# Twelve of 256 elementwise products moved from VectorE to GpSimd in an attention kernel with a bias

## The chip, the cores and the metric

One core of one Trainium2 chip. The metric is device time in microseconds (us) of one execution. A run's time is a little longer than the span of its profile (254.24 against 252.5 in the profiled run of the kernel before), which goes from the first to the last instruction. Engines: TensorE (PE; its weight loads are PEld), VectorE (DVE), ScalarE (ACT), GpSimd (POOL), SyncE (SP).

## The reference

Attention with an additive bias that all heads share: 4 batches x 8 heads, 1024 positions, head size 64.

```
scores = q @ k^T / 8 + bias            # bias: 1 x 1 x 1024 x 1024
attn   = exp(scores - max) / sum(exp(scores - max))
out    = attn @ v
```

## The kernel before

It uses exp(s + bias) = exp(s) * exp(bias). Scores are made transposed (keys on partitions). A *bank* is one block of 128 keys x 512 queries of one head. There are 512 banks in 32 units of 16 (two heads, one half of the queries, eight key blocks). TensorE makes the scores of three banks (one slot), ScalarE takes exp of a slot in one instruction, VectorE multiplies a pair of banks (both heads, same key block) by exp(bias^T), and TensorE forms the weighted sum with v, 65 columns wide so that the last one sums the weights:

```python
def s_fill(g):                                     # TensorE: scores of one slot
    ps = ps_s.tile([P, 3, HQ], F32, tag="s", name="ps")          # two such buffers in PSUM
    for j, b in enumerate(slots[g]):
        ...
        nc.tensor.matmul(ps[:, j, :], kT[:, kc, :], qT[:, h, qh * HQ:(qh + 1) * HQ], start=True, stop=True)

def s_exp(g):                                      # ScalarE
    n = len(slots[g])
    nc.scalar.activation(e_at(slots[g][0], n), open_ps.pop(("S", g))[:, :n, :], ACTF.Exp, scale=scale)

def mul_pair(b, n=2):                              # VectorE: E = E * exp(bias^T), both in SBUF
    pr, h, qh, kc = banks[b]
    e = e_at(b, n)
    nc.vector.tensor_tensor(e, e, eb[:, qh, kc:kc + 1, :].to_broadcast([P, n, HQ]), op=ALU.mult)

def av_bank(b, tag):                               # TensorE: weighted sum
    ...
    for i in range(QC):
        nc.tensor.matmul(acc[:, i, :], e[:, 0, i * P:(i + 1) * P], vall[:, 2 * pr + h, kc, :], ...)
    ...                                            # after 8 banks, VectorE:
        nc.vector.reciprocal(rs[:], acc[:, :, D:D1])                                  # PSUM
        nc.vector.tensor_tensor(oall[...], acc[:, :, :D], rs[:].to_broadcast(...), op=ALU.mult)   # PSUM, SBUF
```

VectorE also copies the transposed q (times a mask) and k out of PSUM. After the start GpSimd only issues loads (of q, k, v and, once, the bias). The order of every engine's instructions is decided when the kernel is built, by a small model of the engines with fixed costs (`EXP` 427 ns a bank, `MUL` 600, and so on). The order is therefore fixed: each engine works through its list, and a wait holds up what stands behind it (in the changed kernel transposes will wait 7.1 us for scalings that stand behind held products).

The softmax here doesn't subtract the row's maximum and nothing guards it: scores larger than these inputs give would overflow.

Of the kernel before, what the change touches and what calls it, by code (L numbers as in the profile page):

```python
# [11 lines left out]
ALU = mybir.AluOpType  # L12
# [3 lines left out]
def kernel(  # L16
# [15 lines left out]
    nc = tc.nc  # L32
    B, H, S, D = q.shape
    P = 128
# [4 lines left out]
    HQ = S // 2  # L39
# [12 lines left out]
    op = ctx.enter_context(tc.tile_pool(name="op", bufs=2))  # L52
# [7 lines left out]
    eb = consts.tile([P, 2, NCH, HQ], BF)  # L60
# [10 lines left out]
    def load_qk(pr):  # L71
        qr = raw.tile([P, 2, NCH, D], BF, name="qr")
        kr = raw.tile([P, 2, NCH, D], BF, name="kr")
        nc.gpsimd.dma_start(out=kr.rearrange("p t c d -> p t (c d)"), in_=kf[pr])  # L74
        nc.gpsimd.dma_start(out=qr.rearrange("p t c d -> p t (c d)"), in_=qf[pr])  # L75
        raws[pr] = (qr, kr)

    def load_v(pr):
        for t in range(2):
            nc.gpsimd.dma_start(out=vall[:, 2 * pr + t, :, :D], in_=vf[pr, :, t])  # L80

    def transpose_pe(pr, which, half, tag):

        src = raws[pr][which]
        px = ps_x.tile([P, QC, P], BF, tag=tag, name="px")
        for c in range(QC):
            for t in range(2):
                nc.tensor.transpose(px[t * D:(t + 1) * D, c, :], src[:, t, half * QC + c, :], ident[:])  # L88
        if (pr, which) not in trs:
            trs[(pr, which)] = (kvp.tile([P, NCH, P], BF, name="kT") if which else  # L90
                                kvp.tile([P, 2, NCH * P], BF, name="qT"))
        dst = trs[(pr, which)]

        def copy():
            if which == 0:

                nc.vector.tensor_tensor(dst[:, :, half * HQ:(half + 1) * HQ],  # L97
                                        px.rearrange("p c q -> p (c q)").unsqueeze(1).to_broadcast([P, 2, HQ]),
                                        mask[:], op=ALU.mult)
            else:  # L100
                nc.vector.tensor_copy(dst[:, half * QC:(half + 1) * QC, :], px[:])  # L101
        return copy


    banks = [(pr, h, qh, kc) for pr in range(NP) for qh in range(2) for kc in range(NCH) for h in range(2)]
# [6 lines left out]
    def e_at(b, n):  # L112
        if b // ET not in etiles:
            etiles[b // ET] = ep.tile([P, ET, HQ], BF, name="E")
        return etiles[b // ET][:, b % ET:b % ET + n, :]
# [26 lines left out]
    def b_exp(qh, k0):  # L142
        nc.scalar.activation(eb[:, qh, k0:k0 + 4, :], open_ps.pop(("B", qh, k0))[:, :4, :], ACTF.Exp)  # L143

    def mul_pair(b, n=2):
        pr, h, qh, kc = banks[b]
        e = e_at(b, n)
        nc.vector.tensor_tensor(e, e, eb[:, qh, kc:kc + 1, :].to_broadcast([P, n, HQ]), op=ALU.mult)  # L148

    oalls = {}  # L150
    po = {}
# [25 lines left out]
    with tc.manual_schedule():  # L177
# [59 lines left out]

        EXP, EXP0, QK, AV, TP = 427, 45, 216, 170, 350
        MUL, COPYQ, COPYK, EVAC, SEM = 600, 650, 420, 620, 80
        order = [("S", g) for g in range(2, NS)]  # L240
        for at, x in ((5, (0, 0)), (7, (0, 4)), (11, (1, 0)), (13, (1, 4))):
            order.insert(at, ("B",) + x)
# [2 lines left out]
        t_act, t_pe, t_dve = T0 + 900, T0, T0  # L245
# [10 lines left out]
        eb_at = {}  # L256
        exp_at = {0: T0 + 400, 1: T0 + 900, 2: T0 + 900}
        mul_at = {}
        mul_next = 0
        av_order = []  # L260
        for u in range(0, NB, 16):
            if u + 16 < NB:
# [5 lines left out]
        def unit_of(b):  # L268
            return banks[b][:3]
# [41 lines left out]
        def pe_piece():  # L311
            if not pieces:
                return None
            pr, which, half = pieces[0]
            if pr not in raw_at or pr not in raws:
                return None
            i = min(len(filled), NO - 1)
            while order[i][0] != "S":
                i -= 1
            at = slots[order[i][1]][0]  # L320
            if at < (pr - 2) * 32 + 8:
                return None

            left = NCH - av_next % NCH
            busy = x_unit.get(unit_of(av_order[av_next])) if av_next % NCH else None
            tags = sorted((x_free[x], x) for x in x_free if x != busy)
            if busy and left < 4 and at < pr * 32 - 16:
                return None
            if not busy and av_next and at < pr * 32 - 16 and tags[0][0] + SEM < t_pe and len(tags) > 1 and tags[1][0] > t_pe:
                return None  # L330
            free, tag = tags[0]
            ready = max(free + SEM, raw_at[pr])

            def emit(t):
                pieces.pop(0)
                copy = transpose_pe(pr, which, half, tag)
                cost = COPYK if which else COPYQ
                x_free[tag] = 1e12

                def run(t2):  # L340
                    copy()
                    x_free[tag] = t2 + cost
                    piece_end[(pr, which, half)] = t2 + cost
                    if which == 0 and half == 1:
                        if pr + 3 < NP:
                            load_qk(pr + 3)
                            raw_at[pr + 3] = t2 + 7000
                        if pr + 2 < NP:
                            load_v(pr + 2)
                dve_q.append((t + TP + SEM, 0, cost, run))  # L350
            return ready, TP, emit

# [27 lines left out]
        def pe_pick():  # L380
            f = pe_fill()
            best = None
            i = len(filled)
            if f and f[0] <= t_pe:
                return (max(t_pe, f[0]),) + f[1:]
            limit = 1e12
            if f:
                limit = max(f[0], act_end_of(i - 1) - f[1] - 100)
            elif i < NO:
                limit = max(act_end_of(i - 2) + SEM, act_end_of(i - 1) - 750)  # L390
            for c in (pe_piece(), pe_av()):
                if c is None:
                    continue
                start = max(t_pe, c[0])
                if start + c[1] > limit:
                    continue
                if best is None or start < best[0]:
                    best = (start,) + c[1:]
            if f and (best is None or f[0] <= best[0]):
                best = (max(t_pe, f[0]),) + f[1:]  # L400
            return best

        def dve_pick():
            nonlocal mul_next
            c = list(dve_q)
            if mul_next < NB:
                pr, h, qh, kc = banks[mul_next]
                if mul_next + 1 in exp_at and (qh, kc) in eb_at:
                    b = mul_next

                    def run(t):
                        nonlocal mul_next
                        mul_pair(b)
                        mul_at[b] = mul_at[b + 1] = t + MUL
                        mul_next += 2
                    c.append((max(exp_at[b + 1], eb_at[(qh, kc)]) + SEM, 2, MUL, run))
            if not c:
                return None
            return min(c, key=lambda x: (max(x[0], t_dve + 100), x[1]))

        def act_pick():
            i = len(act_end)
            if i >= len(filled):
                return None
            return max(t_act, filled[i] + SEM), cost_act(i), i

        while len(act_end) < NO or av_next < NB or dve_q:
            c = []
            a, d, p = act_pick(), dve_pick(), pe_pick()
            if a:  # L430
                c.append((a[0], 0))
            if d:
                c.append((max(t_dve, d[0]), 1))
            if p:
                c.append((p[0], 2))
            t, who = min(c)
            if who == 0:
                i = a[2]
                item = order[i]
                t_act = t + a[1]  # L440
                act_end.append(t_act)
                if item[0] == "S":
                    s_exp(item[1])
                    for b in slots[item[1]]:
                        exp_at[b] = t_act
                else:
                    b_exp(item[1], item[2])
                    for kc in range(4):
                        eb_at[(item[1], item[2] + kc)] = t_act
            elif who == 1:  # L450
                if d in dve_q:
                    dve_q.remove(d)
                t_dve = t + d[2]
                d[3](t)
            else:
                t_pe = t + p[1]
                p[2](t)
# [30 lines left out]
```

## Time and profile before

| | before |
|---|---|
| median of 3 runs | 253.62 us (253.6 to 253.69) |
| busy, of a span of 252.5 us | ACT 95%, PE 91%, DVE 90%, POOL 21% |

The head of the profile's page, with busy time and share of each engine:

```profile
PE 229.4 (91%) x3090; PEld 141.6 (56%) x3144; DVE 226.3 (90%) x461; ACT 239.1 (95%) x180; POOL 52.6 (21%) x72
```

The table of stretches. Columns: from:to, length, busy us (and instructions) of PE, PEld, DVE, ACT and POOL, granted clock of TensorE, DMA share, GB/s:

```profile
120.00:140.00 20.00, 18.93 (x269) 11.32 (x271) 19.20 (x39) 20.00 (x17) 5.99 (x8) 1.00 0.58 81
```

ScalarE is busy for all of the 20 us, as in every such stretch from 20 to 240 us, and VectorE for 19.2, at most 19.4. The groups of instructions, with busy us, mean ns of one, and idle time before them:

```profile
L130 ACT ACTIVATE E<-ps 128x1536 bf16<-128x1536 f32 (+2 forms) x172 | 230.1, 1668 | 2.1 <-PE ps L125 2.1
L148 DVE TENSOR_TENSOR E<-E,eb 128x1024 bf16<-128x1024 bf16 x256 | 163.5, 683 | 1.0 <-ACT eb L143 1.0
```

The list of waits, ACT and then PE (us in total, times, longest):

```profile
ACT E L130 <- PE ps L125: 2.1, 3, 0.9
```

```profile
PE po L160 <- DVE E L148: 1.0, 5, 0.3
```

(The means of ScalarE's groups count the overlap of one exponential with the next, so compare its busy times.) ScalarE never waits after the first 20 us. The end of the run, from the timeline (start, length):

```profile
243.42 1.32 ACT L130 ACTIVATE E<-ps 128x1024 bf16<-128x1024 f32 x1
...
244.47 3.09 DVE L148 TENSOR_TENSOR E<-E,eb 128x1024 bf16<-128x1024 bf16 x5
...
248.72 0.42 DVE L171 TENSOR_TENSOR oall<-po,rs 128x256 f32<-128x256 f32 x1
```

ScalarE's last exponential ends at 244.74 (243.42 + 1.32). VectorE still has five products then, and the run ends 7.73 us later. I call this stretch the *tail*.

Pairing each product with its exponential in the trace, six to nine pairs wait for VectorE through most of the run.

### The profile page before, as it was taken

What the parts mean: (1) busy time and instruction counts of PE and PEld (TensorE: products, weight loads), DVE (VectorE), ACT (ScalarE), POOL (GpSimd) and SP (SyncE); (2) the same over time, 40 slices, a digit from 0 to 9 for tenths busy, and PEclk for the clock granted to TensorE, in tenths of its full rate; (3) what the DMA queues carried; (4) which work ended last, traced back from release to release, by engine and by line L of the source; (5) the groups of instructions that cost most, each with busy time, mean ns of one, the idle gap of its engine ahead of it and who ended that gap; (6) DMA issues with size and microseconds to landing.
All of it is one profiled execution on the core that took longest, in us unless ns stands there. A gap on an engine that the chain in (4) does not pass through costs nothing.

```text
span 252.5 us, 7217 instructions
## 1 busy us (share of the span) xinstructions
PE 229.4 (91%) x3090; PEld 141.6 (56%) x3144; DVE 226.3 (90%) x461; ACT 239.1 (95%) x180; POOL 52.6 (21%) x72
## 2 busy tenths in 40 slices
PE   7768999999999999999999999999999999999982
PEld 2346646665565566565555566565555655555651
DVE  5319799999999999999999999999999999999993
ACT  3899999999999999999999999999999999999970
POOL 6652445022310513013042204034000000000000
PEclk9999999999999999999999999999999999999998
DMA  7999999749291589439196904939020201111112
GB/s 147 171 214 187 191 138 161 90 106 104 66 148 40 105 67 150 64 71 139 42 141 47 187 8 95 118 85 166 5 84 3 86 0 44 44 43 44 49 36 83
DMA packets 47744, 23.79 MB, mean 94 GB/s; under 512 B 34401, under 2 KB 43361, under 8 KB 47457
## 3 DMA queue, kind: packets, MB, share of 16 engines
q0 software_dynamic: 42272, 14.42, 52.7%
q1 hardware_dynamic: 5296, 8.78, 9.6%
q8 instruction: 24, 0.39, 0.7%
q10 hardware_dynamic: 144, 0.13, 0.2%
q14 instruction: 8, 0.06, 0.1%
HBM read 29.36 MB, written 8.39 MB: 150 GB/s over the span
## 4 chain that ended last, share of the span: by engine, by line
PE 44%; ACT 35%; DVE 10%; DMA 4%; issue 3%; POOL 1%; ACTq 1%
ACT E L130 33%; PE ps L125 30%; PE po L160 8%; DVE E L148 6%; PE px L88 6%; DMA qr<-in_q_dram 4%; ACT eb L143 2%; DVE oall L171 1%; DVE qT L97 1%; POOL vall L80 1%; DVE mask L199 1%; DVE rs L170 1%; ACTq L130 1%; PE pb L138 0%; POOL kr L74 0%
## 5 line engine op out<-in xcount | busy, mean ns | idle before, releaser
L130 ACT ACTIVATE E<-ps 128x1536 bf16<-128x1536 f32 (+2 forms) x172 | 230.1, 1668 | 2.1 <-PE ps L125 2.1
L148 DVE TENSOR_TENSOR E<-E,eb 128x1024 bf16<-128x1024 bf16 x256 | 163.5, 683 | 1.0 <-ACT eb L143 1.0
L125 PE MATMUL ps<-qT,kT 128*128 128x512 bf16 x458 | 134.5, 378 | 12.9 <-ACT E L130 4.7
L160 PEld LDWEIGHTS <-E 128*128 128x128 bf16 x2048 | 84.7, 98 | 40.3 <-DVE E L148 2.6
L160 PE MATMUL po<-vall,E 128*128 128x65 bf16 x2048 | 96.4, 194 | 2.4 <-DVE E L148 1.0
L125 PEld LDWEIGHTS <-kT 128*128 128x128 bf16 x512 | 45.3, 96 | 43.1 <-issue 10.2
L74 POOL DMA_DIRECT2D kr<-in_k_dram x15 | 10.5, 699 | 96.4 <-PE px L88 91.5
L171 DVE TENSOR_TENSOR oall<-po,rs 128x256 f32<-128x256 f32 x64 | 27.2, 425 | 2.4 <-DVE rs L170 0.3
L80 POOL DMA_DIRECT2D vall<-in_v_dram x32 | 28.1, 882 | 6.0 <-DMA btraw<-in_bias_dram 4.0
L97 DVE TENSOR_TENSOR qT<-px,mask 128x1024 bf16<-128x1024 bf16 x31 | 21.3, 688 | 2.3 <-PE px L88 1.6
L101 DVE COPY kT<-px 128x512 bf16<-128x512 bf16 x31 | 13.1, 424 | 10.5 <-PE px L88 9.7
L75 POOL DMA_DIRECT2D qr<-in_q_dram x15 | 10.7, 716 | 17.3 <-PE px L88 16.7
L170 DVE RECIPROCAL rs<-po 128x4 f32<-128x4 f32 x64 | 11.4, 179 | 3.1 <-PE po L160 2.7
L88 PE MATMUL px<-ident,qr 128*64 128x128 bf16 x248 | 12.8, 224 | 1.0 <-DMA qr<-in_q_dram 0.9
L88 PE MATMUL px<-ident,kr 128*64 128x128 bf16 x248 | 12.8, 225 | 0.2
L88 PEld LDWEIGHTS <-kr 128*64 128x64 bf16 x248 | 7.9, 109 | 8.5 <-issue 5.2
L88 PEld LDWEIGHTS <-qr 128*64 128x64 bf16 x248 | 8.0, 109 | 8.2 <-issue 6.4
L143 ACT ACTIVATE eb<-pb 128x2048 bf16<-128x2048 bf16 x4 | 7.5, 1881 | 0.6 <-PE pb L138 0.6
L138 PE MATMUL pb<-ident,btraw 128*128 128x128 bf16 x64 | 4.6, 225 | 0.9 <-ACT E L130 0.7
L138 PEld LDWEIGHTS <-btraw 128*128 128x128 bf16 x64 | 4.5, 147 | 1.5 <-issue 1.2
L209 PE MATMUL wm<-zeros 128*128 128x512 bf16 x8 | 3.4, 607 | 1.2 <-DVE zeros L184 1.2
L209 PEld LDWEIGHTS <-zeros 128*128 128x128 bf16 x8 | 1.0, 142 | 2.9 <-issue 1.6
(27 smaller groups left out, 13.3 us busy)
## 6 DMA issues: line engine op xcount, KB each, us to landing
out_dram<-oall SPq DMA_DIRECT2D x32, 256.0 KB, 2.5
vall<-in_v_dram POOLq DMA_DIRECT2D x32, 128.0 KB, 6.0
kr<-in_k_dram POOLq DMA_DIRECT2D x15, 256.0 KB, 4.2
qr<-in_q_dram POOLq DMA_DIRECT2D x15, 256.0 KB, 5.2
btraw<-in_bias_dram POOLq DMA_DIRECT2D x2, 1024.0 KB, 12.6
k0f<-in_k_dram SPq DMA_DIRECT2D x2, 128.0 KB, 3.3
q0f<-in_q_dram ACTq DMA_DIRECT2D x1, 128.0 KB, 2.5
q0f<-in_q_dram SPq DMA_DIRECT2D x1, 128.0 KB, 2.6
```

Of the source, the lines that this page charges most:

```text
L75: nc.gpsimd.dma_start(out=qr.rearrange("p t c d -> p t (c d)"), in_=qf[pr])
L80: nc.gpsimd.dma_start(out=vall[:, 2 * pr + t, :, :D], in_=vf[pr, :, t])
L88: nc.tensor.transpose(px[t * D:(t + 1) * D, c, :], src[:, t, half * QC + c, :], ident[:])
L97: nc.vector.tensor_tensor(dst[:, :, half * HQ:(half + 1) * HQ], px.rearrange("p c q -> p (c q)").unsqueeze(1).to_broadcast([P, 2, HQ]), ma ...
L101: nc.vector.tensor_copy(dst[:, half * QC:(half + 1) * QC, :], px[:])
L125: nc.tensor.matmul(ps[:, j, :], kT[:, kc, :], qT[:, h, qh * HQ:(qh + 1) * HQ], start=True, stop=True)
L130: nc.scalar.activation(e_at(slots[g][0], n), open_ps.pop(("S", g))[:, :n, :], ACTF.Exp, scale=scale)
L143: nc.scalar.activation(eb[:, qh, k0:k0 + 4, :], open_ps.pop(("B", qh, k0))[:, :4, :], ACTF.Exp)
L148: nc.vector.tensor_tensor(e, e, eb[:, qh, kc:kc + 1, :].to_broadcast([P, n, HQ]), op=ALU.mult)
L160: nc.tensor.matmul(acc[:, i, :], e[:, 0, i * P:(i + 1) * P], vall[:, 2 * pr + h, kc, :], start=(kc == 0 and i == 0), stop=(kc == NCH - 1), ...
L170: nc.vector.reciprocal(rs[:], acc[:, :, D:D1])
L171: nc.vector.tensor_tensor(oall[:, qh * QC:(qh + 1) * QC, :], acc[:, :, :D], rs[:].to_broadcast([P, QC, D]), op=ALU.mult)
```

## The change

Its intent: VectorE is always behind, GpSimd is nearly free, so when at least three pairs wait in the model, GpSimd makes the product of the newest of them. The model gives it 2.1 us.

```diff
-    def mul_pair(b, n=2):
+    def mul_pair(b, n=2, eng=nc.vector):
...
-        nc.vector.tensor_tensor(e, e, eb[...].to_broadcast([P, n, HQ]), op=ALU.mult)
+        eng.tensor_tensor(e, e, eb[...].to_broadcast([P, n, HQ]), op=ALU.mult)
...
+        POOLMUL = 2100
+        pool_has = set()
+        t_pool = 30000.0
...
+        def pool_pick():
+            b, n, last = mul_next, 0, None
+            while b + 1 in exp_at and banks[b][2:] in eb_at:
+                if b not in pool_has and max(exp_at[b + 1], eb_at[banks[b][2:]]) <= max(t_pool, t_dve):
+                    n, last = n + 1, b
+                b += 2
+            if n < 3:
+                return None
+            b = last
+            def emit(t):
+                mul_pair(b, eng=nc.gpsimd)
+                pool_has.add(b)
+                mul_at[b] = mul_at[b + 1] = t + POOLMUL
+            return max(t_pool, t_dve - MUL, exp_at[b + 1] + SEM), POOLMUL, emit
...                                   # VectorE skips pairs in pool_has; loads add 2.2 us to t_pool
```

More of the change, by code (lines that the diff above doesn't have):

```diff
@@ L143, in b_exp @@
         nc.scalar.activation(eb[:, qh, k0:k0 + 4, :], open_ps.pop(("B", qh, k0))[:, :4, :], ACTF.Exp)
-    def mul_pair(b, n=2):
+    def mul_pair(b, n=2, eng=nc.vector):
         pr, h, qh, kc = banks[b]
         e = e_at(b, n)
-        nc.vector.tensor_tensor(e, e, eb[:, qh, kc:kc + 1, :].to_broadcast([P, n, HQ]), op=ALU.mult)
+        eng.tensor_tensor(e, e, eb[:, qh, kc:kc + 1, :].to_broadcast([P, n, HQ]), op=ALU.mult)
     oalls = {}
@@ L340, in run @@
                 def run(t2):
+                    nonlocal t_pool
                     copy()
@@ L346, in run @@
                             load_qk(pr + 3)
+                            t_pool = max(t_pool, t2) + 2200
                             raw_at[pr + 3] = t2 + 7000
@@ L349, in run @@
                             load_v(pr + 2)
+                            t_pool = max(t_pool, t2) + 2200
                 dve_q.append((t + TP + SEM, 0, cost, run))
@@ L401, in pe_pick @@
             return best
+        def pool_pick():
[12 more added lines that the diff above has]
+            return max(t_pool, t_dve - MUL, exp_at[b + 1] + SEM), POOLMUL, emit
         def dve_pick():
             nonlocal mul_next
+            while mul_next in pool_has:
+                mul_next += 2
             c = list(dve_q)
@@ L435 @@
                 c.append((p[0], 2))
+            g = pool_pick()
+            if g:
+                c.append((g[0], 3))
             t, who = min(c)
@@ L454 @@
                 d[3](t)
+            elif who == 3:
+                t_pool = t + g[1]
+                g[2](t)
             else:
```

## The prediction

> **What bounds the kernel now.** ScalarE. The busy shares are ACT 95%, PE 91%, DVE 90%, POOL 21%, and the table of stretches shows ACT busy 20.00 of every 20 us from 20 to 240 us. Its 171 score exponentials and 4 bias exponentials follow one another without a gap to 244.7 us; in the list of waits ACT lost only some 6 us, nearly all before 20 us. So no work taken from VectorE can shorten the body. What VectorE alone decides is the tail: in the timeline ACT ends at 244.7, five products (128x1024, one each 0.60 us) run from 244.47 to 247.56, the last reciprocal and scaling end at 249.1, and the output transfer at 252.5. With no products left over at ACT's end, the tail could be about 2 us shorter. That is the most that the change can win: about 251.5 us, 0.8%.
>
> **What VectorE's state is.** Pairing each product with its exponential in the timeline, 6 to 9 pairs wait through most of the run (lag about 5 us at 50 us, 7 us at 200 us), falling to 3 or 4 at the end, once the q and k copies stop after about 170 us. VectorE is almost saturated: 19.1 to 19.4 of 20 us busy. About a quarter of the pairs are read by TensorE within 0.6 us of being made, so there is little slack.
>
> **What the change does.** It removes about 12 of 256 products from VectorE (12 x 0.60 = 7 us) and puts them on GpSimd, whose work in this trace is DMA issues of 0.7 to 0.9 us; the schedule assumes 2.1 us for one. TensorE's order moves a little. If the two engines ran side by side, the lag at the end would shrink, and the time would be 251.5 to 253.5 us.
>
> **Why I expect a loss.** The Trainium skill, "SBUF — State Buffer", section "Who interferes with whom", says that a VectorE instruction with two SBUF inputs contends with a GpSimd instruction that reads SBUF, and that the loser blocks for the whole instruction. Both forms of the product read E and eb from SBUF. No record of this trace shows it: GpSimd reads no tensor in the body. If it holds, each GpSimd product blocks VectorE for about 2.1 us (the schedule's figure; the page "GPSIMD Engine Reference", section 3.1, gives about 2.6 cycles per element for two inputs, hence 2.2 us as an estimate) and saves it 0.60: some 1.5 us lost each, 12 to 18 us in all. The schedule models no blocking, so TensorE, in order, waits at its next weighted sums, and ScalarE, with only two score buffers, waits after it: I estimate 0.7 to 0.9 us of ACT idle for each, some 6 to 11 us in all, less what VectorE's 4% idle absorbs.
>
> **Prediction.** 260 us, range 251.5 to 267. Faster by over 2%: 0.02; within 2%: 0.38; slower by over 2%: 0.60.
>
> **What would show it.** Right: beside each GpSimd product a VectorE product of 2 to 3 us instead of 0.68; VectorE's busy time up by 10 us or more, though it has 12 products fewer; TensorE's wait for E (now 1.0 us) and ACT's wait for score matmuls (now 2.1 us) up by several us each; ACT's busy time unchanged at 239 us. Wrong: VectorE's products stay at 683 ns on average, DVE busy falls to about 219 us, ACT stays gapless, and only the tail after ACT's last exponential changes.
>
> **What would make it wrong.** The engines share less strictly than the page says, or VectorE wins and GpSimd's product stretches to 4 us or more, hidden by the lag; the GpSimd products fall where VectorE works from PSUM; or the dozen lies in a few places where ScalarE's and TensorE's slack swallows the delay.

## The result, and the profile after

The changed kernel takes 266.94 us (median of 6; 265.91 to 269.61), the kernel before 253.66 (median of 6; 253.6 to 256.3): 5.1% slower, ratio 1.0513, 95% interval 1.045 to 1.0576. A ratio here is the mean time of one kernel's fast runs over that of the other's in the same rounds, so it is not quite the ratio of the medians. The direction was predicted. The size was not: 6.4 us of loss forecast, 13.3 measured.

The head of the page, of a span of 265.2 us:

```profile
PE 230.4 (87%) x3144; PEld 140.3 (53%) x3144; DVE 238.2 (90%) x449; ACT 240.8 (91%) x180; POOL 79.8 (30%) x84
```

VectorE has twelve products fewer (449 instructions instead of 461) and is busy 11.9 us longer. The groups:

```profile
L130 ACT ACTIVATE E<-ps 128x1536 bf16<-128x1536 f32 (+2 forms) x172 | 231.9, 1499 | 15.5 <-PE ps L125 12.5 <-issue 2.3 <-ACT E L130 0.5
L148 DVE TENSOR_TENSOR E<-E,eb 128x1024 bf16<-128x1024 bf16 x244 | 176.6, 761 | 4.0 <-ACT E L130 2.5 <-ACT eb L143 1.0
...
L148 POOL TENSOR_TENSOR E<-E,eb 128x1024 bf16<-128x1024 bf16 x12 | 26.8, 2236 | 56.0 <-ACT E L130 42.5 <-issue 13.6
```

A GpSimd product took 2.24 us on average, as the schedule had assumed. VectorE's own products rose from 683 to 761 ns on average. Their median is unchanged at 684 ns, and exactly twelve of the 244 are longer than 0.9 us: they take 2.01 to 2.60 us, 18.8 us more in all than twelve ordinary ones. Where they lie is seen in the timeline of all engines from 44 us on, around the first GpSimd products (its `x3` row is three of them in a row):

```profile
47.14 7.27 POOL L148 TENSOR_TENSOR E<-E,eb 128x1024 bf16<-128x1024 bf16 x3 [5.50 <-ACT E L130]
...
47.49 0.42 DVE L171 TENSOR_TENSOR oall<-po,rs 128x256 f32<-128x256 f32 x1
...
47.83 2.07 DVE L148 TENSOR_TENSOR E<-E,eb 128x1024 bf16<-128x1024 bf16 x1
...
49.82 0.68 DVE L97 TENSOR_TENSOR qT<-px,mask 128x1024 bf16<-128x1024 bf16 x1
...
50.42 5.14 DVE L148 TENSOR_TENSOR E<-E,eb 128x1024 bf16<-128x1024 bf16 x3
...
52.49 0.66 PE L160 MATMUL po<-vall,E 128*128 128x65 bf16 x16 [1.59 <-DVE E L148]
...
53.84 1.45 ACT L130 ACTIVATE E<-ps 128x1536 bf16<-128x1536 f32 x1 [1.41 <-PE ps L125]
...
58.67 1.45 ACT L130 ACTIVATE E<-ps 128x1536 bf16<-128x1536 f32 x1 [3.38 <-PE ps L125]
```

At 47.14 GpSimd starts. VectorE's scaling of the outputs at 47.49, whose big input is in PSUM, takes its usual 0.42 us, and so does the q copy at 49.82 (0.68). But the product at 47.83 needs 2.07 us, and the three from 50.42 need 5.14 us instead of 1.9. TensorE has waited 1.59 us for E when it goes on at 52.49, and ScalarE idles 1.41 us before 53.84 and 3.38 us before 58.67. The two engines' own timelines later on, VectorE and then GpSimd, show that it works in both directions:

```profile
67.20 3.13 DVE L148 TENSOR_TENSOR E<-E,eb 128x1024 bf16<-128x1024 bf16 x2
...
73.01 0.68 DVE L148 TENSOR_TENSOR E<-E,eb 128x1024 bf16<-128x1024 bf16 x1
73.75 0.42 DVE L101 COPY kT<-px 128x512 bf16<-128x512 bf16 x1
74.09 2.74 DVE L148 TENSOR_TENSOR E<-E,eb 128x1024 bf16<-128x1024 bf16 x2
```

```profile
67.05 2.13 POOL L148 TENSOR_TENSOR E<-E,eb 128x1024 bf16<-128x1024 bf16 x1 [2.68 <-ACT E L130]
73.21 2.47 POOL L148 TENSOR_TENSOR E<-E,eb 128x1024 bf16<-128x1024 bf16 x1 [4.04 <-ACT E L130]
```

At 67.05 GpSimd is first and takes 2.13 us, and VectorE's product of 67.20 stretches until 69.7. At 73.21 a VectorE product (73.01 to 73.69) is first: GpSimd's takes 2.47 us, about the 0.4 us of waiting longer, and VectorE's next product at 74.09 is held until GpSimd is done. So whichever product comes second waits for the rest of the other. In the trace each of the twelve held VectorE products ends 0.55 us after its GpSimd product, though they started 0.15 to 1.11 us after it: they are held to its end, not merely slowed. The profile counts that waiting as busy time, which is why VectorE "works" more with less to do.

The waits, ACT and PE:

```profile
ACT E L130 <- PE ps L125: 12.5, 13, 3.4
```

```profile
PE po L160 <- DVE E L148: 10.8, 18, 1.8
PE px L88 <- DVE oall L171: 7.1, 6, 2.4
```

ScalarE waits for score matmuls six times as long as before (12.5 us, not 2.1). TensorE waits for E (10.8 us instead of 1.0) and also for the scaling of outputs, which frees a PSUM tile for its transposes and stands behind the held products in VectorE's list. Adding up ScalarE's gaps in the trace gives 13.4 us after 20 us, none of it in the kernel before. (Next to the run e1 below ScalarE ends 15.0 us later, 1.6 us more than the gaps: in a row the exponentials overlap and start every 1.34 us, while one after a gap takes 1.45 us, so each of the 15 gaps loses another 0.1 us.) TensorE's granted clock fell once. Two stretches around that place, in the columns of the table of stretches (the clock is the third number from the end):

```profile
51.97:55.39 3.42, 1.31 (x19) 0.70 (x19) 3.42 (x3) 1.91 (x2) 2.46 (x2) 1.00 0.00 0
55.39:62.20 6.81, 6.03 (x56) 3.67 (x57) 5.88 (x11) 2.77 (x2) 3.16 (x3) 0.50 0.45 116
```

TensorE was busy for only 1.31 of the 3.42 us before, then was granted half its clock for 6.8 us. All six runs have a mean clock of 0.981 to 0.986, against 0.992 to 0.999 in the recorded runs of the kernel before. The tail, last:

```profile
256.68 2.56 ACT L130 ACTIVATE E<-ps 128x1536 bf16<-128x1536 f32 x2
...
261.41 0.42 DVE L171 TENSOR_TENSOR oall<-po,rs 128x256 f32<-128x256 f32 x1
```

From ScalarE's last exponential, which ends at 259.24, to the end of the span are 5.9 us instead of 7.7: this small gain is there.

### The profile page after: what moved, and what is told of

Its sections match the earlier page's. It is cut to its first block, busy times and chain, and to the rows that moved or that the text cites. A ratio compares the mean times of both kernels' runs of the same rounds, so it can differ in the third digit from the quotient of the medians.

```text
span 265.2 us, 7283 instructions
## 1 busy us (share of the span) xinstructions
PE 230.4 (87%) x3144; PEld 140.3 (53%) x3144; DVE 238.2 (90%) x449; ACT 240.8 (91%) x180; POOL 79.8 (30%) x84
## 4 chain that ended last, share of the span: by engine, by line
PE 35%; DVE 33%; ACT 29%; issue 2%; ACTq 0%
ACT E L130 26%; DVE E L148 23%; PE ps L125 21%; PE po L160 8%; PE px L88 5%; DVE oall L171 3%; DVE qT L97 3%; ACT eb L143 3%; DVE rs L170 1%; DVE kT L101 1%; DVE mask L199 1%; DVE qT L225 0%; PE px L224 0%; ACTq L130 0%; DVE qT L197 0%
## 5 line engine op out<-in xcount | busy, mean ns | idle before, releaser
L130 ACT ACTIVATE E<-ps 128x1536 bf16<-128x1536 f32 (+2 forms) x172 | 231.9, 1499 | 15.5 <-PE ps L125 12.5
L148 DVE TENSOR_TENSOR E<-E,eb 128x1024 bf16<-128x1024 bf16 x244 | 176.6, 761 | 4.0 <-ACT E L130 2.5
L125 PE MATMUL ps<-qT,kT 128*128 128x512 bf16 x512 | 140.1, 381 | 7.5 <-ACT E L130 4.0
L160 PE MATMUL po<-vall,E 128*128 128x65 bf16 x2048 | 96.6, 195 | 12.6 <-DVE E L148 10.8
L125 PEld LDWEIGHTS <-kT 128*128 128x128 bf16 x512 | 43.8, 97 | 37.1 <-issue 8.3
L148 POOL TENSOR_TENSOR E<-E,eb 128x1024 bf16<-128x1024 bf16 x12 | 26.8, 2236 | 56.0 <-ACT E L130 42.5
L75 POOL DMA_DIRECT2D qr<-in_q_dram x15 | 10.8, 719 | 23.6 <-PE px L88 22.9
```

Of the source, the lines that this page charges most:

```text
L148: eng.tensor_tensor(e, e, eb[:, qh, kc:kc + 1, :].to_broadcast([P, n, HQ]), op=ALU.mult)
```

## The experiments

**Two kinds of start.** Runs of most of these kernels come in two groups about 2.5 us apart (before: 253.6 to 254.2, or 256.2 to 256.3). The profile tells which is which: the group of score matmuls between 5 and 20 us, for the kernel before (254.24 us in its profiled run) and for the run called e4_memset below (256.28 us):

```profile
L125 PE MATMUL ps<-qT,kT 128*128 128x512 bf16 x21 | 6.4, 380 | 2.6 <-ACT E L130 1.5 <-DVE qT L225 1.0
```

```profile
L127 PE MATMUL ps<-qT,kT 128*128 128x512 bf16 x21 | 8.0, 499 | 2.3 <-ACT E L132 1.3 <-DVE qT L235 1.0
```

In the later starters these matmuls take 499 to 506 ns on average instead of 380. The clock records of the traces agree: the first full clock stands at 3.9 to 6.2 us in the nine early starters among the profiled runs, at 13.5 to 13.9 us in the five late ones (e2, e3, e4, e5, e7). Runs without a profile are sorted by their time alone. I compare runs of the same start where it matters, and say so.

Theory A: GpSimd's product shuts VectorE's out, VectorE's lateness passes through TensorE to ScalarE. Rival B: the new order of the instructions costs the time. Rival C: GpSimd's products come too late for TensorE. Rivals D and E, on the cluster of the first four, appear further down.

### e1_left_out: the dozen not made at all

The changed kernel, wrong result (relative error 0.022).

```diff
-                mul_pair(b, eng=nc.gpsimd)
                 pool_has.add(b)
```

> The changed kernel's order of instructions, with the dozen products left out altogether (wrong result on purpose). Theory A (GpSimd's product shuts VectorE's out): without a GpSimd product nothing is shut out, VectorE's products are back at 0.68 us each, ACT has no gaps after 20 us, and the dozen's relief shows in the tail: 251 to 253 us. Rival B (the new order of TensorE's and VectorE's work costs the time): 258 us or more. Rival C (GpSimd's products come too late for TensorE): 251 to 253 us, as A.

Measured: 251.9 us (251.85 to 252.11), ratio 0.9912, interval 0.9865 to 0.9958.

```profile
PE 230.8 (92%) x3144; PEld 140.5 (56%) x3144; DVE 220.0 (88%) x449; ACT 239.1 (96%) x180; POOL 52.6 (21%) x72
```

VectorE's busy time falls to 220.0 us. ScalarE has no gap after 20 us, no product is long, and the tail is 5.91 us. Rival B falls: this is the order of the changed kernel. It also prices the wish: a dozen products for nothing gain 1.8 us, and the GpSimd products cost 266.9 - 251.9 = 15.0 us.

### e2_vector: the dozen on VectorE, in the same places

```diff
-                mul_pair(b, eng=nc.gpsimd)
+                mul_pair(b)
```

> The changed kernel's order, the dozen products made by VectorE at the place where the schedule hands them to GpSimd. Theory A: near the kernel before, 253 to 256 us, since a product out of turn delays the older ones by 0.6 us only. Rival B: 258 us or more. Rival C: 253 to 256 us.

Measured: 254.77 us, and 257.08 to 257.11 in three runs (ratio 1.0084, interval 1.001 to 1.0157); the profiled one of these is a late starter. The median, 257.09, lies in none of the ranges that I had given, which did not allow for late starts. Against runs of the same start the order costs about 1 us (254.77 against 253.7, 257.09 against 256.25), with five small gaps of ScalarE between 52 and 116 us, 1.86 us in all. So the order matters a little, but not 13 us.

### e3_shadow: GpSimd products that nobody reads, added to the kernel before

```diff
+    scr = consts.tile([P, 2, HQ], BF)
...
+    SHADOW = (60, 62, 68, 80, 96, 108, 168, 198, 270, 300, 366, 396)   # where the change hands out its own
+
+    def shadow(b):
+        qh, kc = banks[b][2:]
+        e = e_at(b, 2)
+        nc.gpsimd.tensor_tensor(scr[:], e, eb[:, qh, kc:kc + 1, :].to_broadcast([P, 2, HQ]), op=ALU.mult)
...
+                        if b in SHADOW:
+                            shadow(b - 2)
                         mul_pair(b)
```

> The kernel before, unchanged in all its work and order, plus 12 GpSimd products of the same size into a tile that nobody reads, each handed out at the place where the changed kernel hands out its own. Nobody waits for them. Theory A: twelve VectorE products of 2.0 to 2.6 us beside them, VectorE busy time up by about 19 us, ACT idle 12 to 18 us after 20 us, 264 to 272 us: at least as slow as the change, as nothing is taken from VectorE. Rivals B and C: 253.6 us, within 1 us.

Measured: 272.47 us (271.8 to 273.74), ratio 1.0725, interval 1.0664 to 1.0787.

```profile
L149 DVE TENSOR_TENSOR E<-E,eb 128x1024 bf16<-128x1024 bf16 x256 | 184.8, 765 | 1.0 <-ACT eb L144 1.0
...
L156 POOL TENSOR_TENSOR scr<-E,eb 128x1024 bf16<-128x1024 bf16 x12 | 27.2, 2265 | 57.9 <-DVE E L149 50.1 <-DVE rs L178 7.8
```

No result, order or wait of the kernel depends on these products, and still it is slower than the change. Twelve VectorE products take 2.06 to 2.62 us, 21.5 us too much in all. Theory A stands. Rival C is not needed: here nothing comes late from GpSimd, and in the changed kernel's own list of waits no engine waits for a GpSimd product.

### e4_memset: GpSimd as busy, but only writing

```diff
-        nc.gpsimd.tensor_tensor(scr[:], ...)
+        nc.gpsimd.tensor_copy(scr[:, :1], e[:, 0, :1])     # fixes the time
+        nc.gpsimd.memset(big[:], 0.0)                       # 128 x 2048 float32
```

> As e3, but each GpSimd product replaced by a one-column copy (which fixes its time) and a memset of 2048 float32, which reads nothing and keeps GpSimd busy for some 1.5 to 2.5 us. If VectorE is shut out of a read interface, as the Trainium skill says for a product with two SBUF inputs, the memset leaves it alone: 253.6 to 254.5 us, VectorE's products at 0.68 us. If GpSimd's being busy, or any of its SBUF traffic, is what costs, it is as slow as e3, over 262 us.

(The page meant is "SBUF — State Buffer", section "Who interferes with whom".)

Measured: 253.74 us (253.56 to 256.28), ratio 1.0006, interval 0.994 to 1.0072.

```profile
L150 DVE TENSOR_TENSOR E<-E,eb 128x1024 bf16<-128x1024 bf16 x256 | 163.3, 682 | 1.0 <-ACT eb L145 1.0
...
L158 POOL MEMSET big<- 128x2048 f32 x12 | 21.6, 1804 | 0.0
```

Memsets of 1.80 us, each beside two to four of VectorE's products, leave these at 682 ns. GpSimd being busy, or only writing SBUF, costs nothing here. The cost lies in what e3 adds: a GpSimd instruction that reads two SBUF tensors and writes one. None that only reads was tried.

### e5_first4, e6_last8 and e7_spread: which of the dozen costs what

```diff
 e5:
-            if n < 3:
+            if n < 3 or len(pool_has) >= 4:
 e6:
-                mul_pair(b, eng=nc.gpsimd)
+                mul_pair(b, eng=nc.gpsimd if len(pool_has) >= 4 else nc.vector)
 e7:
+        last_pick = [0.0]
...
-            if n < 3:
+            if n < 3 or max(t_pool, t_dve) < last_pick[0] + 8500:
...
+                last_pick[0] = t
```

> Only the first four products (three of them one after another near 47 us) go to GpSimd, all others stay on VectorE. Theory A with all its parts: four blocks, about 6 us of ACT idle time between 50 and 65 us, with TensorE's granted clock halved for some 7 us there, as in the changed kernel: 257 to 261 us. Rival D (each block costs the same 1.25 us wherever it lies, and the halved clock costs nothing): 4 blocks cost 5 us, less the shorter tail of the later schedule if it appears: 256 to 258 us.

> The changed kernel's order, but the first four of the dozen are made by VectorE, so that eight single products stay on GpSimd, 6 to 48 us apart. Theory A: 8 blocks of VectorE of about 1.6 us, ACT idle some 1.1 us after each, no halved clock after 20 us: 261 to 264 us. If the cluster of the first four carries most of the loss (rival E): 256 to 259 us.

> The same rule, but at least 8.5 us between two GpSimd products, which leaves eleven single ones from 48 to 210 us. Theory A: eleven blocks at about 1.1 us each over the 251.9 us of the kernel with the dozen left out: 262 to 266 us, and no halved clock after 20 us[...]. Rival E (the cluster and its halved clock are most of the loss): 255 to 259 us.

Measured: e5 257.55 us (three runs 257.19 to 257.74; the profiled one, 260.95, a late starter), e6 262.85 us (262.2 to 263.5), e7 264.22 us (three runs 264.07 to 264.29; the profiled one, 266.53, a late starter). Ratios 1.0161 (unclear at 2%), 1.0331 and 1.0415.

Eleven single products cost (264.2 - 251.9) / 11 = 1.12 us each, with no halved clock between the start and the end in the profiled run; e6's eight cost (262.85 - 254.77) / 8 = 1.0 us each, measured from the one early run of e2. The first four cost (257.4 - 251.9) / 4 = 1.4 us each, and the clock is halved for 6.8 us at the same place as in the changed kernel. At 1.12 us each, twelve would cost 13.4 of the 15.0 us, so some 1.6 us are left for the cluster with its halved clock; from e5 it is 5.5 - 4 x 1.12 = 1.0 us. Rival E falls: it asked for 259 us or less in e6 and e7. Rival D's figure for e5 (256 to 258 us) is met as well as A's, so e5 alone does not decide between them; e7 beside e5 speaks against it. One part of A's expectation failed: in the profiled run of e6 (263.5 us, the longest of its four) the clock was halved for 3.4 us at 162 us, after one single product. What the halved clock alone costs, no run here separates from the waits around it; when it comes is taken up in the last section.

### e3h_shadow_half and e3q_shadow_quarter: shorter GpSimd products

As e3, with 128x512 and 128x256 elements.

```diff
-        nc.gpsimd.tensor_tensor(scr[:], e, eb[:, qh, kc:kc + 1, :].to_broadcast([P, 2, HQ]), op=ALU.mult)
+        nc.gpsimd.tensor_tensor(scr[:, 0, :], e[:, 0, :], eb[:, qh, kc, :], op=ALU.mult)                                # half
+        nc.gpsimd.tensor_tensor(scr[:, 0, :HQ // 2], e[:, 0, :HQ // 2], eb[:, qh, kc, :HQ // 2], op=ALU.mult)           # quarter
```

> As e3 (the kernel before, plus 12 GpSimd products that nobody reads), but each of half the columns, 128x512, about 1.1 us long. Theory A: a VectorE product is held for what is left of the GpSimd product, so it takes 0.7 to 1.7 us instead of 2.0 to 2.6, the excess over 0.68 us falls from 21 us in all to 8 to 11 us, and the time to 258 to 264 us. If a block had a fixed price, whatever the length of the GpSimd product: 270 us or more, as e3.

> As e3 and e3h, with GpSimd products of a quarter of the columns, 128x256. The 12 blocks of e3 (1.79 us of excess each) cost about 18 us, those of e3h (0.82 us each) about 5.2 us: a line through the two says that some 0.4 us of each block is swallowed and the rest passed on in full. If that is so, blocks of 0.2 to 0.45 us are swallowed nearly whole: 253.4 to 254.6 us in the runs that start fast. If a share of each block (half) is passed on instead, 12 x 0.35 x 0.5 gives 255.5 us or more.

Measured: half 258.97 us (258.8 to 261.52), ratio 1.0211, interval 1.0143 to 1.0278; quarter 254.11 us (253.86 to 256.55), ratio 1.0029, interval 0.9974 to 1.0085. The groups of the half, then of the quarter:

```profile
L149 DVE TENSOR_TENSOR E<-E,eb 128x1024 bf16<-128x1024 bf16 x256 | 173.2, 720 | 1.0 <-ACT eb L144 1.0
```

```profile
L149 DVE TENSOR_TENSOR E<-E,eb 128x1024 bf16<-128x1024 bf16 x256 | 167.6, 699 | 1.0 <-ACT eb L144 1.0
```

Per GpSimd product, with runs of the same start compared (e3: its profiled run, 273.13, a late starter with no halved clock between the start and the end, less 256.25. Its two runs of 271.8, with a mean clock of 0.985, look like early starters with a halved clock and would give 1.50 us each. The others: the mean of their early starters less that of the kernel before in the same rounds):

| GpSimd product | VectorE products too long by, each | time added, each | swallowed |
|---|---|---|---|
| 128x1024, 2.27 us | 21.5 / 12 = 1.79 us | 16.9 / 12 = 1.41 us | 0.38 us |
| 128x512, 1.30 us | 9.88 / 12 = 0.82 us | 5.15 / 12 = 0.43 us | 0.39 us |
| 128x256, 0.81 us | 4.1 / 12 = 0.34 us | 0.29 / 12 = 0.02 us | 0.32 us |

So with this order and these places the kernel swallows 0.3 to 0.4 us of each block and passes on the rest in full. A share passed on in proportion (half of each) would have cost 2 us in the last row. The change agrees: (18.8 - 15.0) / 12 = 0.3 us. With the other places of e7 it is more: (18.2 - 12.3) / 11 = 0.5 us. Why it is this much was not tested.

### e8_fold8, e9_fold12 and e10_fold3: relieving VectorE by another engine

No GpSimd product. For a few pairs late in the run TensorE adds the bias in PSUM, and their products are dropped:

```diff
             nc.tensor.matmul(ps[:, j, :], kT[:, kc, :], qT[...], start=True, stop=True)
...
+            if b - b % 2 in FOLD:         # e8: 356 + 18k, k < 8; e9: 356 + 12k, k < 12; e10: 374, 398, 422
+                for i in range(QC):
+                    nc.tensor.matmul(ps[:, j, i * P:(i + 1) * P], btraw[...][:, kc, :], ident8[:],   # 8 x identity
+                                     start=False, stop=True, skip_group_check=True)
...                                   # VectorE skips these pairs; the model adds 320 ns a bank to TensorE
```

> No GpSimd product. The kernel before, but for eight pairs of the last third the bias is added by TensorE in PSUM before the exponential (four more 128-column matmuls a bank, bias rows against 8 times the identity), so that VectorE has eight products fewer (4.8 us) and nobody is shut out. If what the change wanted (relief of VectorE) is worth what the kernel with the dozen left out shows, about 1.8 us of tail, and TensorE has the room late in the run: 251.5 to 252.6 us in the fast starts. If TensorE has no room, ACT waits for score matmuls instead: 254 us or more.

> The same with twelve pairs, every twelfth bank from 356 on, so the dozen of the change given to TensorE. If the tail is the whole gain, no better than e8, 251.5 to 252.6 us; if TensorE runs out of room, ACT waits, and it is slower than e8 by 1 us or more.

> As e8, but three pairs (banks 374, 398 and 422) folded into TensorE instead of eight. e8 and e9 did not make ACT wait, but their time after ACT's last exponential grew from 7.7 us (the kernel before) to 8.6 and 10.5 us, about 0.5 us a pair, as TensorE ended behind. By that line TensorE alone would allow a tail of about 6.2 us at three pairs, and VectorE, with three products fewer, 7.7 less 1.8, about 5.9 us: 252.0 to 252.8 us in the fast starts. If TensorE has no room at all late in the run, 253.6 us or more.

Measured: e8 255.42 us (254.79 to 257.24), ratio 1.0056, interval 1.0011 to 1.0101; e9 257.54 us (256.86 to 259.14), ratio 1.0143, interval 1.0097 to 1.0189; e10 252.96 us (252.78 to 254.55), ratio 0.9967, interval 0.9922 to 1.0013. My expectation for e8 and e9 missed: TensorE had no room for so much, and it showed not as waits of ScalarE (there is no new one after 20 us) but as TensorE's own arrears: the time came out in the range of the second guess for a reason that I had not given. The end of e8, from the timeline:

```profile
247.03 2.00 PE L167 MATMUL po<-vall,E 128*128 128x65 bf16 x60 [0.85 <-DVE oall L178]
...
249.71 0.42 DVE L178 TENSOR_TENSOR oall<-po,rs 128x256 f32<-128x256 f32 x1
```

In e8 sixty weighted-sum matmuls are still due at 247.03, after VectorE's last product (246.4) and a wait of 0.85 us for VectorE's scaling of outputs, and the tail, from ScalarE's end at 244.86, is 8.6 us. In e10 it is 5.92 us (from 245.16), as in e1. Four of its six runs lie between 252.78 and 252.98, below all eleven of the kernel before (253.56 or more), but two are longer and the interval just includes 1. The four lie at or just above the upper end of what I expected. So e10 is probably better by 0.3%, and this is not proven.

## Why the prediction was right or wrong

- *ScalarE bounds the body; the most that the change can win is about 2 us of tail, 251.5 us.* Right: 251.9 us with the dozen for nothing (e1). (The profile counts 172 score exponentials, not 171.) But the shorter tail is no sign of relief in itself: e2 has it too (5.92 us) with all products on VectorE and pays with 1.86 us of gaps earlier. In the profiled runs the tail goes with the order: 5.90 to 5.94 us in all six kernels ordered by the rule (the change, e1, e2, e5, e6, e7), 7.71 to 7.74 us in all five with the order of the kernel before (itself, e3, e3h, e3q, e4), whatever VectorE had lost by then. What in the order sets it was not tested.
- *Each GpSimd product blocks VectorE for about 2.1 us.* Right in kind; in size it was 18.8 / 12 = 1.57 us on average, because the held product started a while after GpSimd's. The reason given was the Trainium skill, "SBUF — State Buffer", section "Who interferes with whom": a VectorE instruction with two SBUF inputs contends with a GpSimd instruction that reads SBUF, and the loser blocks. Traces agree: twelve products of 2.01 to 2.60 us in the change, twelve in e3, none in e4, where GpSimd only writes, and PSUM-fed VectorE instructions keep their length. The same page's statement that an instruction with at most one SBUF input, outside its two-port modes, doesn't contend fits the q copy's 0.68 us beside a GpSimd product.
- *2.1 to 2.2 us for one.* Right: 2.12 us when GpSimd comes first, 2.24 on average. The estimate of 2.2 us had been worked out from the 2.6 cycles per element of the skill's "GPSIMD Engine Reference", section 3.1.
- *Some 1.5 us lost each, 12 to 18 us in all.* A little too high. This was net of the 0.60 us that a product less saves: 18.8 us of holding less 12 x 0.60 is 11.6 us, and VectorE's busy time rose by 11.9 us, about 1 us each.
- *0.7 to 0.9 us of ACT idle for each, 6 to 11 us in all, less what VectorE's 4% idle absorbs.* This is the step that failed: how much of a block reaches ScalarE. ScalarE idled 13.4 us, 1.1 us each, which is more than the whole net loss of VectorE, and it ended 15.0 us later than in e1 (259.24 against 244.27), 15.0 / 12 = 1.25 us each. I had let the saved 0.60 us, the two score buffers and the idle time take more than half off each block of 2.1 us. But the saved 0.60 us buys nothing while ScalarE bounds the body, as my own first step said: in e1, with the dozen for nothing, ScalarE ends only 0.5 us earlier than in the kernel before. And the buffers and the idle time together swallowed only about 0.3 us of 1.57 (0.3 to 0.4 in e3, e3h and e3q, 0.5 in e7). Two errors pulled in opposite directions, the block too long and the part passed on too small, so 6.4 us forecast became 13.3. Why so little was swallowed is not shown; my reading is that the order is fixed, so a pair late at VectorE is late at TensorE, and the six to nine waiting pairs are arrears, not a reserve.
- *Not in the prediction at all:* the halved clock of TensorE after the first cluster. With the cluster itself it is worth about 1.6 us of the 15.0 by the difference between the single products of e7 and the whole, and 1.0 us by e5.
- The sum: 253.7 - 1.8 (tail) + 12 x 1.12 + 1.6 = 266.9 us, against 266.94 measured. The 1.6 is what the other terms leave, so the sum checks only that the terms are complete.
- *The signs to look for.* VectorE busy up by 10 us or more: 11.9. TensorE's wait for E and ScalarE's for scores up by several us: 1.0 to 10.8, and 2.1 to 12.5. ACT's busy time unchanged at 239: 240.8, nearly.

## What to carry to other kernels

Before work is moved to an idle engine, look for what the two engines share: here a GpSimd product of 2.1 us with its inputs in SBUF took more of VectorE's time (about 1.6 us) than the 0.6 us it saved, while GpSimd's memsets took none. In a kernel like this one, whose order is fixed and whose three main engines are all busy for 90% or more, count a block on one of them nearly in full (here, on VectorE, all but 0.3 to 0.5 us), and don't set the work taken away against it, until an experiment shows slack. And price the wish first: a run with the work simply left out says at most what the move can gain (1.8 us here).

## What the Trainium skill lacked or had wrong

- "SBUF — State Buffer", "Who interferes with whom": right, but it doesn't say how the block looks in a profile. The held product's own record is stretched (684 ns to 2.01 to 2.60 us) and counts as busy, so VectorE's busy time rose from 226.3 to 238.2 us with twelve products fewer. "Perfetto Trace Analysis" doesn't say it either.
- The same page says that the second to start blocks, whichever it is. These runs add the two prices: a GpSimd product that comes second takes up to 2.57 us instead of 2.12, so VectorE delays GpSimd by at most the rest of its product, and GpSimd delays VectorE by up to 1.9 us.
- "TensorE: Matmul & The Clock Gate", its closing table "Why this matters for your kernels", advises against TensorE idle gaps over about 3 us. Here the clock was halved from 55.4 us on, for 6.8 us, after one wait of 1.59 us (to 52.49) and 1.6 us into the next (53.80 to 56.17), with 1.31 of 3.42 us busy before it; in e6 it was halved at 162.2 us after one wait of 1.81 us, while e3 had one of 1.87 us (to 55.73) and kept its clock. So gaps well under 3 us are not safe, and the length of a gap alone does not decide. In all fourteen traces the changes of the clock within a run lie whole multiples of 3.41 us apart (51.20, 6.83 and 201.39 us in the change). Cut into such stretches, counted from the first full clock, all 16 stretches at full clock with TensorE busy for at most 41% were followed by a halved clock (most at the end of a run), of the seven with 44 to 47% only e6's was, and of those with 52% or more none.
- The same page says in Part 1 that the warm-up varies from run to run, and that its penalty is under 1% of a typical span. Here late and early starts make two groups of runs about 2.5 us apart, which is 1.0% of 253.6 us. In a comparison at half a per cent the two groups must be told apart, by the first score matmuls (380 or 500 ns).
